# Transformer block, fp32-like matmuls on one core: the first stage written out in a fixed order, and sums over partitions done on four column groups

## The chip, the cores and the metric

The kernel runs on one core of one Trainium2 chip. The metric is the device time in microseconds (us) of one execution; lower is better.

## What is computed

Two layers of a diffusion backbone over 512 latent tokens `x` and 256 context tokens `ctx`, 1024 wide. Cut to what matters here:

```python
silu_c, silu_cc = silu(c), silu(c_ctx)[None]
for i in range(2):                                   # layer 0: attention, layer 1: short conv
    mod   = silu_c  @ ada_w[i] + ada_b[i]            # six vectors of 1024 for the latent tokens
    mod_c = silu_cc @ ada_w[i] + ada_b[i]            # the same for the context
    h  = rmsnorm(x,   norm1_g[i]) * (1 + sc1)  + sh1
    hc = rmsnorm(ctx, norm1_g[i]) * (1 + csc1) + csh1
    y  = diff_attention(h, hc, ...)                  # 8 heads, q, k, v from h; k, v from hc too
    x  = x + g1 * y
    x  = x + g2 * swiglu(rmsnorm(x, norm2_g[i]) * (1 + sc2) + sh2)
return rmsnorm(x, final_g)
```

Only the latent stream is returned, so the context stream is needed for the keys and values of layer 0 alone.

## The kernel before

**Products.** An fp32 operand is split into a high part rounded to fp32r and the fp32r rest (`split`, lines 54 to 56: ACT casts, DVE subtracts), and a product is three fp32r matmuls, high by high, high by low and low by high (`mm3`, lines 78 to 81). Everything stays feature-major: features on partitions, tokens along the free axis.

**First stage** (lines 123 to 313). It loads `x` (four tiles `xn`), `ctx` (two tiles `cn`), the first 2048 columns of `ada_w[0]` (sixteen halves `raw_a`, 512 KB each in two transfers, through a pool of three buffers) and, for each of eight feature blocks k, the 512 columns of `wqkv` that head 0 (q, k) and heads 0 and 1 (v) need (`raw_w`). For each k, `ada0` sums silu(c) and silu(c_ctx) times the block of `ada_w` over all 1024 rows: both halves are split by ACT and DVE into `whi_a` and `wlo_a`, sixteen matmuls `pm` of 256 columns with four weight columns (`cst`) accumulate, ACT copies the four rows to `mr`, two small transposes `pmt` turn them, and DVE makes the gain `A` and shift `m`. `norm_apply` then makes `hx[k]` (`hh`, `hl`) and `hc[k]` (`ch`, `cl`), and the products of block k add to `vps` (v), `qps` and `kps`.

**Attention** (lines 398 to 640). For head 0 `finish_v`, `finish_q` and `finish_k` split v, apply the rotary embedding on DVE (`swq`, `rtq`, `swk`, `rtk`, `qt`, `kt`) and spread q and k over partitions by eight transfers (`qs`, `ks`); then come the score matmuls `S`. Between the heads stand the products of later heads (`psq`, `psk`, `pskc`, `psv`), steps of the modulation vectors (below) and `subnorm`, which sums a head's squares over partitions: four matmuls `pq` with the squares as weights and one column of ones.

**Modulation vectors** (`ada_steps`). The other ten vectors are summed as `acc += silu(c)[k] * ada_w[k rows]` on DVE (tiles `ada`, loads `araw`), then over partitions: the three during attention (`spread_sum` false) by eight one-column matmuls `pada`; the seven during the first FFN (`spread_sum` true) by a split, two times two fp32r matmuls of 512 columns with a matrix of ones, a masked product and a reduction on DVE.

**Order.** The program is written in the order above, but a scheduler that simulates the engines decides where each instruction stands in its engine's queue, and every engine, SP's queue of transfers among them, runs its queue in order. So loads and casts for later heads stand between those of the first stage.

Of the kernel before, what the change touches and what calls it, by code (L numbers as in the profile page):

```python
# [25 lines left out]
def block_kernel(  # L26
# [74 lines left out]
    const.tile([P, 104], F32, name="pad")  # L101
# [20 lines left out]
    for tag, n, bufs in (  # L122
# [3 lines left out]
        + [("sq", 512, 1), ("dg1", 512, 1)]  # L126
# [33 lines left out]

# [38 lines left out]
    def nat_rstd(src, tag, name):  # L199

        nb = len(src)
        ss = ap.tile([P, 8], F32, tag="ss", name=f"ss{name}")
        for t in range(nb):
            for f in range(2):
                junk = ap.tile([P, 512], F32, tag="sq", bufs=1, name=f"junk{name}")
                nc.scalar.activation(
                    junk, src[t][:, f * 512:(f + 1) * 512], AF.Square,
                    accum_out=ss[:, t + 4 * f:t + 4 * f + 1],
                )
# [4 lines left out]
        nc.gpsimd.tensor_tensor(r, v, mhalf[:, :nb], op=ALU.pow)  # L214
        ps = spread(r, nb, "pt", name)
# [17 lines left out]
    def ada0(k, raws):  # L233
        pm = psB.tile([P, 512], F32, tag="pt", name=f"pm{k}")[0:4, 0:256]
        for hf in range(2):
            hi, lo = split_w(raws[hf], 1024, f"a{k}_{hf}")
            for i in range(4):
                kb = 4 * hf + i
                for n, w in enumerate((hi, lo)):
                    nc.tensor.matmul(  # L240
                        pm, cst[:, kb, :], w[:, i * 256:(i + 1) * 256],
                        start=(kb == 0 and n == 0), stop=(kb == DB - 1 and n == 1),
                    )
        mr = ap.tile([4, 256], F32, tag="dg1", bufs=1, name=f"mr{k}")
        nc.scalar.copy(mr, pm)
        pt = psB.tile([P, 512], F32, tag="pt", name=f"pmt{k}")[:, :8].rearrange("p (s c) -> p s c", c=4)
        for s in range(2):
            nc.tensor.transpose(pt[:, s, :], mr[:, s * P:(s + 1) * P], ident[0:4, 0:4])
        nc.vector.reduce_sum(out=m0[:, k], in_=pt.rearrange("p s (m h) -> p s m h", h=2), axis=AX.X)
        nc.vector.tensor_tensor(  # L250
            m0[:, k], m0[:, k], bias0[:, k, :, None].to_broadcast([P, 2, 2]), op=ALU.add
# [4 lines left out]


    XT0 = [ap.tile([P, T], F32, tag=f"Or{k}", bufs=1, name=f"XT{k}") for k in range(DB)]
    rx = nat_rstd(xn, "sw", "x")
    for k in range(0, DB, 2):  # L260
        pt = psB.tile([P, 2, T], F32, tag="S", name=f"ptx{k}")
        for a in range(2):
            for t in range(TB):
                nc.tensor.transpose(pt[:, a, t * P:(t + 1) * P], xn[t][:, (k + a) * P:(k + a + 1) * P], ident)
            nc.vector.tensor_copy(XT0[k + a], pt[:, a, :])
        if k == 0:
            ada0(0, raws0)
    rc = nat_rstd(cn, "ks0", "c")
    ctt = [ap.tile([P, 4, C], F32, tag="araw", name=f"ct{i}") for i in range(2)]
    CT = [ctt[k // 4][:, k % 4, :] for k in range(DB)]  # L270
    for i in range(2):
        pt = psB.tile([P, 4, C], F32, tag="S", name=f"ptc{i}")
        for a in range(4):
            k = 4 * i + a
            for t in range(CB):
                nc.tensor.transpose(pt[:, a, t * P:(t + 1) * P], cn[t][:, k * P:(k + 1) * P], ident)
        for a in (0, 2):
            nc.scalar.copy(ctt[i][:, a:a + 2, :], pt[:, a:a + 2, :])
# [3 lines left out]
    kcps = vps[1][:, 512:768]  # L282
    for k in range(DB):
        raws = raws0 if k == 0 else [load_ada0(k, hf) for hf in range(2)]
        raw = ap.tile([P, 512], F32, tag="e", bufs=3, name=f"raw_w0_{k}")
        qkv = da_wqkv[0, k * P:(k + 1) * P, :].rearrange("p (s c) -> p s c", s=3)
        nc.sync.dma_start(raw[:, 0:256].rearrange("p (s c) -> p s c", s=2), qkv[:, 0:2, 0:P])
        nc.sync.dma_start(raw[:, 256:512], qkv[:, 2, 0:256])
        if k:
            ada0(k, raws)  # L290
        norm_apply(ap, "rt", hx[k], XT0[k], rx, A0[:, k, 0:1], m0[:, k, 0, 0:1], T)
        wh = ap.tile([P, 512], F32R, tag="pth", bufs=3, name=f"w0h_{k}")
        wl = ap.tile([P, 512], F32R, tag="ptl", bufs=3, name=f"w0l_{k}")
        nc.scalar.copy(wh, raw)
# [647 lines left out]
```

## Time and profile before

| | us |
|---|---|
| median of three runs (lowest, highest) | 1350.98 (1350.11, 1352.2) |
| profiled execution | 1350.57 |
| its span, first to last instruction | 1348.8 |
| PE busy in it (share) | 1302.2 (97%) |
| DVE, ACT, POOL busy | 786.4, 501.8, 97.2 |

The span is what the trace covers; 1.8 us of the profiled time lie outside it. A busy PE means that some matmul was in flight, not that it ran at its peak.

### The profile page before, as it was taken

The page shows a single profiled execution, that of the slowest core. Times are in us where ns is not written, and L with a number is a line of the kernel's source. Part 1 is how long each engine was busy: PE and PEld are TensorE (multiplying, and loading weights), DVE is VectorE, ACT ScalarE, POOL GpSimd, SP SyncE. Part 2 cuts the span into 40 slices and gives each one's busy share as a digit, 9 for nine tenths or more (in the row PEclk, how much of TensorE's full clock was granted, in tenths as well). Part 3 has the DMA queues.
Part 4 walks back from the last instruction along what each step waited for, and adds up shares of the span by engine and source line. Part 5 has one row for each costly group of instructions (what it writes and reads, how often), then busy time and mean ns, then how long its engine had stood idle before and what let it go on. Part 6 is the DMA issues. An engine that isn't in the chain of part 4 may idle for free.

```text
span 1348.8 us, 17927 instructions
## 1 busy us (share of the span) xinstructions
PE 1302.2 (97%) x7068; PEld 1120.1 (83%) x7068; DVE 786.4 (58%) x1089; ACT 501.8 (37%) x841; POOL 97.2 (7%) x103
## 2 busy tenths in 40 slices
PE   6788999999999999999999999999999999999997
PEld 5568899999789888888788899888898888888887
DVE  6787989888867677767642265444563333332222
ACT  7534455545556333322222253222452223222122
POOL 2100000000014000000000050000420000000000
PEclk9998999999999999999999999999999999999999
DMA  9865755623532677667633323333233333333321
GB/s 301 259 202 146 207 126 172 156 64 96 153 110 84 184 218 218 207 214 218 210 102 102 101 65 110 94 102 101 79 94 94 99 104 94 94 91 113 100 72 63
DMA packets 238742, 182.79 MB, mean 136 GB/s; under 512 B 6937, under 2 KB 220226, under 8 KB 238658
## 3 DMA queue, kind: packets, MB, share of 16 engines
q1 hardware_dynamic: 238658, 181.65, 45.6%
q8 instruction: 55, 0.90, 0.3%
q14 instruction: 29, 0.24, 0.1%
HBM read 162.75 MB, written 4.19 MB: 124 GB/s over the span
## 4 chain that ended last, share of the span: by engine, by line
PE 82%; DMA 9%; DVE 5%; ACT 2%; issue 1%; SPq 1%; POOL 1%; DVEq 0%; ACTq 0%; POOLq 0%
PE po_fo L81 6%; PE po_fo L79 6%; PE po_fo L80 6%; DMA araw<-in_ada_w_dram 5%; PE pb L80 5%; PE pb L79 5%; PE pb L81 5%; PE pa L80 5%; PE pa L79 5%; PE pa L81 5%; PE S L511 3%; DMA raw_a<-in_ada_w_dram 2%; DVE ada L365 2%; PE pt L532 1%; PE psv L80 1%; PE psv L81 1%
## 5 line engine op out<-in xcount | busy, mean ns | idle before, releaser
L55 ACT CAST whi_f<-raw_f 128x1024 fp32r<-128x1024 f32 x87 | 91.4, 1051 | 232.7 <-issue 118.2
L56 DVE TENSOR_TENSOR wlo_f<-raw_f,whi_f 128x1024 fp32r<-128x1024 f32 x87 | 107.4, 1234 | 77.9 <-ACT whi_f L55 75.0
L56 DVE TENSOR_TENSOR wlo_fo<-raw_fo,whi_fo 128x1024 fp32r<-128x1024 f32 (+1 forms) x48 | 54.5, 1135 | 118.2 <-ACT whi_fo L55 116.8
L79 PE MATMUL po_fo<-uh,whi_fo 128*128 128x512 f32 (+1 forms) x324 | 118.7, 366 | 0.1
L80 PE MATMUL po_fo<-ul,whi_fo 128*128 128x512 f32 (+1 forms) x324 | 118.6, 366 | 0.0
L81 PE MATMUL po_fo<-uh,wlo_fo 128*128 128x512 f32 (+1 forms) x324 | 118.4, 365 | 0.0
L365 DVE SCALAR_TENSOR_TENSOR ada<-araw,sil,ada 128x1024 f32<-128x1024 f32 x70 | 90.1, 1287 | 47.4 <-DMA araw<-in_ada_w_dram 47.2
L55 ACT CAST whi_fo<-raw_fo 128x1024 fp32r<-128x1024 f32 (+1 forms) x48 | 47.1, 981 | 177.6 <-PE po_fo L80 142.3
L784 DVE TENSOR_TENSOR uu<-sl,pb 128x512 f32<-128x512 f32 (+1 forms) x48 | 30.7, 640 | 81.2 <-PE pb L81 76.7
L81 PE MATMUL pb<-h2h,wlo_f 128*128 128x512 f32 (+1 forms) x192 | 71.7, 374 | 0.0
L79 PE MATMUL pa<-h3h,whi_f 128*128 128x512 f32 (+1 forms) x192 | 71.5, 373 | 0.0
L80 PE MATMUL pb<-h2l,whi_f 128*128 128x512 f32 (+1 forms) x192 | 71.4, 372 | 0.0
L79 PE MATMUL pb<-h2h,whi_f 128*128 128x512 f32 (+1 forms) x192 | 71.4, 372 | 0.0
L81 PE MATMUL pb<-h3h,wlo_f 128*128 128x512 f32 (+1 forms) x192 | 71.3, 371 | 0.0
L80 PE MATMUL pb<-h3l,whi_f 128*128 128x512 f32 (+1 forms) x192 | 71.3, 371 | 0.0
L79 PE MATMUL pb<-h3h,whi_f 128*128 128x512 f32 (+1 forms) x192 | 71.3, 371 | 0.0
L81 PE MATMUL pa<-h3h,wlo_f 128*128 128x512 f32 (+1 forms) x192 | 71.3, 371 | 0.0
L80 PE MATMUL pa<-h3l,whi_f 128*128 128x512 f32 (+1 forms) x192 | 71.1, 371 | 0.0
L79 PEld LDWEIGHTS po_fo<-uh,whi_fo 128*128 128x128 f32 x324 | 61.1, 189 | 10.4 <-DVE on L871 0.3
L80 PEld LDWEIGHTS po_fo<-ul,whi_fo 128*128 128x128 f32 x324 | 61.1, 189 | 10.0
L81 PEld LDWEIGHTS po_fo<-uh,wlo_fo 128*128 128x128 f32 x324 | 61.1, 189 | 9.7
L519 ACT ACTIVATE e<-S,mx 128x768 f32<-128x768 f32 x64 | 58.1, 908 | 23.8 <-DVE mx L515 17.9
(337 smaller groups left out, 3462.9 us busy)
## 6 DMA issues: line engine op xcount, KB each, us to landing
raw_f<-in_ffn_w_in_dram SPq DMA_DIRECT2D x88, 512.0 KB, 3.7
araw<-in_ada_w_dram SPq DMA_DIRECT2D x80, 512.0 KB, 4.4
raw_fo<-in_ffn_w_out_dram SPq DMA_DIRECT2D x32, 512.0 KB, 3.6
raw_a<-in_ada_w_dram SPq DMA_DIRECT2D x32, 256.0 KB, 4.6
qs<-qt SPq DMA_DIRECT2D x32, 256.0 KB, 5.0
raw_wv<-in_da_wqkv_dram SPq DMA_DIRECT2D x12, 512.0 KB, 3.3
ks<-kt SPq DMA_DIRECT2D x32, 192.0 KB, 5.0
raw_fo<-in_ffn_w_out_dram SPq DMA_DIRECT2D x16, 384.0 KB, 3.2
```

The source lines that it names most:

```text
L55: nc.scalar.copy(hi, src)
L56: nc.vector.tensor_tensor(lo, src, hi.bitcast(F32), op=ALU.subtract)
L79: nc.tensor.matmul(ps, sh, mh, start=start, stop=False)
L80: nc.tensor.matmul(ps, sh, ml, start=False, stop=False)
L81: nc.tensor.matmul(ps, sl, mh, start=False, stop=stop)
L365: nc.vector.scalar_tensor_tensor(acc, raw, s, acc, op0=ALU.mult, op1=ALU.add)
L511: nc.tensor.matmul(S[:, a:b], q[m][:, j, qb * P:(qb + 1) * P], ks[m][:, a:b], start=(j == 0), stop=(j == 1),)
L519: nc.scalar.activation(em, S[:, :KV], AF.Exp, bias=mx[:, m:m + 1], accum_out=den[:, m, qb:qb + 1])
L532: nc.tensor.transpose(pt[:, i * P:(i + 1) * P], e[0][:, k * P:(k + 1) * P], ident)
L784: nc.vector.tensor_tensor(u, s, pb, op=ALU.mult)
```

## The change

Four parts. (1) `ada0` becomes `ada0_sums` and `ada0_columns`: no split; `cst` holds fp32 weights padded from 2 to 32 columns, and eight plain fp32 matmuls of 256 columns write four groups of 32 PSUM partitions, feature block i of each half to group i; two matmuls with a 0/1 matrix `pick` then add the four groups and turn the result. The raw halves go round nine buffers (the three of `raw` and the six of `whi` and `wlo`). (2) The stage is inside `manual_schedule` for PE, DVE, ACT and SP: its instructions keep the order in which they are written (context products one block behind the latent ones), the loads stand in the order of use, and the transfers that only later stages need are issued after the last load of `raw_w`. Instructions of later stages may still stand between. DVE makes the low part of `raw_w`, which POOL made; ACT copies four of the eight `XT` tiles. (3) `ada_steps` sums over partitions by four fp32 matmuls of 256 columns on four groups, an ACT copy `sada`, and two transposes, in both places. (4) `subnorm` does the same with 128 columns, a copy `sums` and one transpose. `finish_q` and `finish_k` are written ahead of `finish_v`.

```diff
-    def load_ada0(k, hf):
-        raw = wp.tile([P, 1024], F32, tag="raw", name=f"raw_a{k}_{hf}")
+    def load_ada0(i):
+        k, hf = divmod(i, 2)
+        raw = wp.tile([P, 1024], F32, tag=("raw", "whi", "wlo")[i % 3], bufs=nw, name=f"raw_a{k}_{hf}")
...
+    fixed = ExitStack()
+    fixed.enter_context(tc.manual_schedule(engines={
+        mybir.EngineType.PE, mybir.EngineType.DVE, mybir.EngineType.Activation, mybir.EngineType.SP
+    }))
...
-        pm = psB.tile([P, 512], F32, tag="pt", name=f"pm{k}")[0:4, 0:256]
+        pm = psB.tile([P, 512], F32, tag="pt", name=f"pm{k}")[:, 0:256]
         for hf in range(2):
-            hi, lo = split_w(raws[hf], 1024, f"a{k}_{hf}")
             for i in range(4):
-                kb = 4 * hf + i
-                for n, w in enumerate((hi, lo)):
-                    nc.tensor.matmul(
-                        pm, cst[:, kb, :], w[:, i * 256:(i + 1) * 256],
-                        start=(kb == 0 and n == 0), stop=(kb == DB - 1 and n == 1),
-                    )
+                nc.tensor.matmul(
+                    pm[32 * i:32 * i + 32, :], cst[:, 4 * hf + i, :], raws[2 * k + hf][:, i * 256:(i + 1) * 256],
+                    start=(hf == 0), stop=(hf == 1),
+                )
...
+        while len(raws) < min(2 * k + 11, 2 * DB):
+            raws.append(load_ada0(len(raws)))
...
     for k in range(DB):
+        if k + 1 < DB:
+            split_w0(k + 1)
+        mr = ada0_sums(k + 1) if k + 1 < DB and k != 1 else None
         for t in range(TB):
+            values(vps[0], hx, t, k)
+        if mr is not None:
+            ada0_columns(k + 1, mr)
+            latent(k + 1)
         for o, ps in ((0, qps), (P, kps)):
+            columns(k, o, ps, hx)
...
+        if k >= LAG:
+            context_products(k - LAG)
+            context(k - LAG + 1)
...
+    with tc.issue_after(last_w.ins):
...
         for k in range(DB):
             nc.sync.dma_start(xt_dram[k], XT0[k])
...
-        hi, lo = (pool.tile([P, D], F32R, tag="araw", name=f"ada{n}{l}_{j}") for n in "hl")
-        split(hi, lo, acc)
...
+        for g in range(4):
+            nc.tensor.matmul(
+                ps[32 * g:32 * g + 32, 0:256], ones_f[:, 0:32], acc[:, g * 256:(g + 1) * 256],
+                start=True, stop=True,
+            )
+        sums = pool.tile([P, 256], F32, tag="dg1", bufs=1, name=f"sada{l}_{j}")
+        nc.scalar.copy(sums, ps[:, 0:256])
+        for n in range(2):
+            nc.tensor.transpose(ps[:, 256 + n * P:256 + (n + 1) * P], sums[:, n * P:(n + 1) * P], ident)
...
         for t in range(n):
             nc.tensor.matmul(
-                ps[:, t:t + 1], sq[:, t * P:(t + 1) * P], ones_f[:, 0:1], start=True, stop=True
+                ps[32 * t:32 * t + 32, 0:P], ones_f[:, 0:32], sq[:, t * P:(t + 1) * P], start=True, stop=True
             )
+        sums = ap.tile([P, P], F32, tag="sums", bufs=1, name=f"sums{h}")
+        nc.scalar.copy(sums[:32 * n], ps[:32 * n, 0:P])
```

The order moves in three places that matter below. First PE's queue around block 3 of the first stage, before:

```order
L248 MATMUL pmt_528<-ident,mr_526 128x4 x2
L240 MATMUL pm_582<-whi_a_0_583,cst 4x256
L240 MATMUL pm_582<-wlo_a_0_584,cst 4x256
...
L79 MATMUL vps_365<-w0h_538,hh_139 128x256
L80 MATMUL vps_365<-w0l_539,hh_139 128x256
L79 MATMUL qps<-hh_139,w0h_538 128x512
L79 MATMUL kps<-hh_139,w0h_538 128x512
L79 MATMUL vps_366<-w0h_538,ch_155 128x256
L80 MATMUL vps_366<-w0l_539,ch_155 128x256
L240 MATMUL pm_582<-wlo_a_1_596,cst 4x256
```

and of the change, at block 4 (`hh_144`, `hl_145` are its parts):

```order
L260 MATMUL pm_644<-raw_a_0_346,cst 32x256 x4
L260 MATMUL pm_644<-raw_a_1_382,cst 32x256 x4
L79 MATMUL vps_360<-w0h_582,hh_144 128x256
L80 MATMUL vps_360<-w0l_583,hh_144 128x256
L81 MATMUL vps_360<-w0h_582,hl_145 128x256
...
L273 MATMUL pmt_667<-pick,mr_653 128x2 x2
L79 MATMUL qps<-hh_144,w0h_582 128x512
```

The sums of one block stand in a piece ahead of the products of the block before, where they were strewn between them. Second, SP's queue of transfers at the end of the first stage, before (the last `raw_a` and what follows):

```order
L360 DMA araw_2_0_1113<-in_ada_w_dram 128x1024
L153 DMA raw_a_0_897<-in_ada_w_dram 128x4x128 x2
L153 DMA raw_a_1_900<-in_ada_w_dram 128x4x128 x2
L70 DMA raw_wq_1268<-in_da_wqkv_dram 128x8x128
L360 DMA araw_2_1_1149<-in_ada_w_dram 128x1024
L70 DMA raw_wk_1274<-in_da_wqkv_dram 128x8x128
```

and of the change, where `...` stands for seven more `xt_spill` and eight small loads:

```order
L154 DMA raw_a_1_539<-in_ada_w_dram 128x4x128 x2
L70 DMA raw_wq_1136<-in_da_wqkv_dram 128x8x128
L165 DMA raw_w_7_586<-in_da_wqkv_dram 128x2x128
L166 DMA raw_w_7_586<-in_da_wqkv_dram 128x256
L392 DMA rcos<-in_rope_cos_dram 128x512
L396 DMA lamr<-in_da_lambda_dram 128x256
L401 DMA xt_spill<-XT_241 128x512
...
L436 DMA araw_2_0_981<-in_ada_w_dram 128x1024
L70 DMA raw_wk_1142<-in_da_wqkv_dram 128x8x128
L70 DMA raw_wv_0_1255<-in_da_wqkv_dram 128x4x256
L436 DMA araw_2_1_1017<-in_ada_w_dram 128x1024
```

All spills of `XT` and the small loads now stand between the last weights of the first stage and the first `araw`. Third, DVE's queue at the same place, of the change (`hl_149` and `hl_151` are the low parts of blocks 6 and 7, `swq_887` is the first step of q of head 0):

```order
L439 TENSOR_SCALAR ada_2_980<-araw_2_0_981,sil 128x1024
L246 SCALAR_TENSOR_TENSOR hl_149<-na,m_239,hh_148 128x512
...
L441 SCALAR_TENSOR_TENSOR ada_2_980<-araw_2_1_1017,sil,ada_2_980 128x1024
L274 TENSOR_TENSOR m_239<-pmt_777,V_226 128x4
...
L441 SCALAR_TENSOR_TENSOR ada_2_980<-araw_2_2_1077,sil,ada_2_980 128x1024
L246 SCALAR_TENSOR_TENSOR hl_151<-na,m_239,hh_150 128x512
...
L441 SCALAR_TENSOR_TENSOR ada_2_980<-araw_2_3_1113,sil,ada_2_980 128x1024
L477 TENSOR_TENSOR swq_887<-qps,rsin 128x512
```

Four steps of the vector `ada_2` stand ahead of `swq`, one of them ahead of each of the last two low parts; before, six steps stood ahead of it. Between the steps that are shown stand two `raw` casts' subtractions (`wlo_wk`, `wlo_wv_0`) too.

## Rows read from the trace of the kernel before

**Rows 1.** Windows by stage: us and busy us (instructions) per engine, granted clock, DMA share, GB/s.

```profile
0.00:86.00 86.00, 64.09 (x416) 49.88 (x416) 63.54 (x115) 48.67 (x85) 15.52 (x16) 0.98 0.85 267
86.00:108.00 22.00, 15.67 (x73) 13.13 (x73) 16.75 (x30) 5.49 (x11) 0.00 (x0) 0.89 0.71 195
108.00:450.00 342.00, 336.21 (x2252) 307.32 (x2253) 288.51 (x478) 177.19 (x358) 27.14 (x31) 0.99 0.48 132
450.00:1348.80 898.80, 886.27 (x4330) 749.78 (x4328) 417.56 (x468) 270.43 (x389) 54.57 (x56) 1.00 0.41 123
```

**Rows 2.** Groups of instructions up to 108 us: busy us, mean ns, idle time before.

```profile
L56 DVE TENSOR_TENSOR wlo_a<-raw_a,whi_a 128x1024 fp32r<-128x1024 f32 x16 | 20.0, 1252 | 8.1 <-ACT whi_a L55 7.9
...
L55 ACT CAST whi_a<-raw_a 128x1024 fp32r<-128x1024 f32 x16 | 16.6, 1044 | 12.1 <-DMA raw_a<-in_ada_w_dram 11.4 <-PE pm L240 0.6
```

**Rows 3.** Waits of SP's queue up to 110 us: in total, times, longest.

```profile
SPq L153 <- DVE wlo_a L56: 7.2, 5, 2.3
```

**Rows 4.** Windows of the loading, columns as in the first group.

```profile
4.00:28.00 24.00, 16.37 (x99) 12.10 (x100) 16.00 (x35) 18.18 (x41) 7.46 (x5) 1.00 1.03 345
28.00:48.00 20.00, 16.61 (x110) 13.48 (x108) 14.46 (x22) 12.25 (x18) 3.21 (x2) 0.91 0.94 279
```

**Rows 5.** Timeline of PE: start, us, line, shapes, count, [idle before].

```profile
29.51 0.40 PE L81 MATMUL kps<-hh,w0l 128*128 128x512 f32 x1
29.74 0.28 PE L79 MATMUL vps<-w0h,ch 128*128 128x256 f32 x1
29.86 0.28 PE L80 MATMUL vps<-w0l,ch 128*128 128x256 f32 x1
29.97 0.28 PE L240 MATMUL pm<-whi_a,cst 128*4 128x256 f32 x1
30.09 0.28 PE L81 MATMUL vps<-w0h,cl 128*128 128x256 f32 x1
```

**Rows 6.** Timeline of PE later: plain fp32 matmuls and transposes.

```profile
127.04 0.49 PE L532 MATMUL pt<-ident,e 128*128 128x128 f32 x3
...
128.06 1.62 PE L372 MATMUL pada<-ones_f,ada 128*128 128x1 f32 x14
...
418.48 1.02 PE L586 MATMUL pn<-nsq,ones_f 128*128 128x256 f32 x4
```

**Rows 7.** Instructions on the tile `pada` in the first FFN: ns min, median, max.

```profile
L385 PE MATMUL pada<-adah,ones_r x14: 397/404/496, 464.6 to 681.0; 128*128 128x512 f32 x14
```

**Rows 8.** Timeline of SP's queue: start, us in the queue, transfer, count.

```profile
18.68 0.85 SPq L326 DMA_DIRECT2D xt_spill<-XT  x2
...
66.99 0.34 SPq L360 DMA_DIRECT2D araw<-in_ada_w_dram  x1
...
96.65 3.22 SPq L420 DMA_DIRECT2D qs<-qt  x4
99.92 3.90 SPq L420 DMA_DIRECT2D ks<-kt  x4
```

**Rows 9.** Timeline of DVE: steps of the vector `ada`, then head 0.

```profile
58.24 0.75 DVE L363 TENSOR_SCALAR ada<-araw,sil 128x1024 f32<-128x1024 f32 x1 [0.96 <-DMA araw<-in_ada_w_dram]
...
70.90 1.69 DVE L365 SCALAR_TENSOR_TENSOR ada<-araw,sil,ada 128x1024 f32<-128x1024 f32 x1 [0.56 <-DMA araw<-in_ada_w_dram]
...
82.94 1.28 DVE L365 SCALAR_TENSOR_TENSOR ada<-araw,sil,ada 128x1024 f32<-128x1024 f32 x1 [1.50 <-DMA araw<-in_ada_w_dram]
...
87.28 0.68 DVE L408 TENSOR_TENSOR swq<-qps,rsin 128x512 f32<-128x512 f32 x1
...
99.44 0.69 DVE L56 TENSOR_TENSOR kt<-rtk,kt 128x512 fp32r<-128x512 f32 x1
```

**Rows 10.** Timeline of PE at the first scores.

```profile
107.98 2.90 PE L511 MATMUL S<-ks,qs 128*128 128x512 f32 x8 [3.71 <-issue]
```

**Rows 11.** Windows at the first scores, columns as in the first group.

```profile
107.00:110.00 3.00, 2.02 (x6) 1.76 (x7) 2.13 (x5) 1.80 (x3) 0.00 (x0) 0.50 0.28 90
110.00:115.00 5.00, 5.00 (x30) 4.86 (x29) 4.55 (x7) 1.76 (x4) 0.00 (x0) 0.68 0.74 166
```

More of the change, by code (lines that the diff above doesn't have):

```diff
@@ L268, in block_kernel, with split_w0, values @@
-    rc = nat_rstd(cn, "ks0", "c")
+    W0 = {}
+    def split_w0(k):
+        raw, W0[k, "dma"] = raw0[k]
+        wh = ap.tile([P, 512], F32R, tag="pth", bufs=3, name=f"w0h_{k}")
+        wl = ap.tile([P, 512], F32R, tag="ptl", bufs=3, name=f"w0l_{k}")
+        split(wh, wl, raw)
+        W0[k] = wh, wl
+        if len(raw0) < DB:
+            raw0.append(load_w0(len(raw0)))
+    def values(ps, h, t, k):
+        wh, wl = W0[k]
+        mm3(
+            ps[:, t * 256:(t + 1) * 256], h[k][0][:, t * P:(t + 1) * P], h[k][1][:, t * P:(t + 1) * P],
+            wh[:, 256:512], wl[:, 256:512], k == 0 and t % 2 == 0, k == DB - 1 and t % 2 == 1,
+        )
@@ new lines, in columns, with latent, context, context_products @@
+    def columns(k, o, ps, h):
+        wh, wl = W0[k]
+        mm3(ps, wh[:, o:o + P], wl[:, o:o + P], h[k][0], h[k][1], k == 0, k == DB - 1)
+    def latent(k):
+        norm_apply(ap, "rt", hx[k], XT0[k], rx, A0[:, k, 0:1], m0[:, k, 0, 0:1], T)
+    def context(k):
+        norm_apply(ap, "rt", hc[k], CT[k], rc, A0[:, k, 1:2], m0[:, k, 0, 1:2], C)
+    def context_products(k):
+        for t in range(CB):
+            values(vps[1], hc, t, k)
+        columns(k, P, kcps, hc)
+    XT0 = [ap.tile([P, T], F32, tag=f"Or{k}", bufs=1, name=f"XT{k}") for k in range(DB)]
@@ L269, in block_kernel @@
+    nc.vector.tensor_copy(XT0[6], ptx[6])
+    nc.vector.tensor_copy(XT0[0], ptx[0])
+    r = rstd_of(ssx, TB, "x")
+    for k in (2, 4):
+        nc.vector.tensor_copy(XT0[k], ptx[k])
+    for k in (7, 1, 3, 5):
+        nc.scalar.copy(XT0[k], ptx[k])
+    rx = spread_out(r, TB, "sw", "x")
+    split_w0(0)
+    mr = ada0_sums(0)
+    ada0_columns(0, mr)
+    latent(0)
     ctt = [ap.tile([P, 4, C], F32, tag="araw", name=f"ct{i}") for i in range(2)]
     CT = [ctt[k // 4][:, k % 4, :] for k in range(DB)]
[L271 to L278, printed above, removed]
@@ L282, in block_kernel @@
     kcps = vps[1][:, 512:768]
+    ptc = vps[1].rearrange("p (a c) -> p a c", c=C)
+    LAG = 1
     for k in range(DB):
[L284 to L294, printed above, removed]
-        nc.gpsimd.tensor_tensor(wl, raw, wh.bitcast(F32), op=ALU.subtract)
-        for t in range(TB):
-            mm3(
-                vps[0][:, t * 256:(t + 1) * 256],
-                hx[k][0][:, t * P:(t + 1) * P], hx[k][1][:, t * P:(t + 1) * P],
-                wh[:, 256:512], wl[:, 256:512], k == 0 and t % 2 == 0, k == DB - 1 and t % 2 == 1,
-            )
@@ L303, in block_kernel @@
-        for o, ps in ((0, qps), (P, kps)):
-            mm3(ps, wh[:, o:o + P], wl[:, o:o + P], hx[k][0], hx[k][1], k == 0, k == DB - 1)
-        norm_apply(ap, "rt", hc[k], CT[k], rc, A0[:, k, 1:2], m0[:, k, 0, 1:2], C)
-        for t in range(CB):
-            mm3(
-                vps[1][:, t * 256:(t + 1) * 256],
-                hc[k][0][:, t * P:(t + 1) * P], hc[k][1][:, t * P:(t + 1) * P],
-                wh[:, 256:512], wl[:, 256:512], k == 0 and t % 2 == 0, k == DB - 1 and t % 2 == 1,
-            )
```

184 lines of the change are left out of this document (105 added, 79 removed).

## The prediction

> **What bounds the kernel now.** I read the windows by stage first [rows 1]. From 108 us, where the first scores start, to the end PE has a matmul in flight for 336.2 of 342.0 us and then for nearly all of the remaining 898.8 us, while DVE stays below it: there the time is PE's work, and whoever hands PE a microsecond less or starts it a microsecond earlier gains it. Ahead of that stands a stretch of 108 us in which PE is busy for 64.1 of 86 and 15.7 of 22 us. This is the stage that the change rewrites. What ends last in it shows in three views. SP's queue waits 7.2 us for DVE's `wlo_a` [rows 3]: a raw half can't be loaded until the split has freed its buffer. The transfers run at 345 GB/s up to 28 us and at 279 up to 48 us [rows 4]. After that stage comes the chain of head 0 on DVE: `swq` at 87.28, the last `kt` ending at 100.13 (99.44 + 0.69) [rows 9], eight transfers whose last issue ends at 103.82 [rows 8], the first score at 107.98, after 3.71 us in which PE does nothing [rows 10].
>
> So the question is when the first score starts in the changed kernel, what PE has behind it by then, and what the new sums cost PE afterwards.
>
> **The sums on PE.** In the kernel before, a 256-column fp32r matmul takes 0.12 us from start to start and a 512-column one 0.23 [rows 5]. A plain fp32 matmul of 256 columns is two records; four records of `pn` take 1.02 us, and with 0.38 us for the last one alone the spacing is (1.02 - 0.38) / 3 = 0.214 us, so 0.43 us for one matmul [rows 6]. Four of them cost 1.71 us if the groups run one after the other, and 0.43 if all four run at once. No row of before shows two column groups at work, so both ends stay. I take a value between: matmuls start in order, the second record of a group needs the same columns as the first and must wait for it, and the next group's first record can run beside it. That makes five slots in place of eight, 1.07 us. Per block of `ada0` (eight matmuls, nine slots) this is 1.9 us, with ends 0.9 and 3.4; before it was 16 x 0.115 = 1.8.
>
> Later sums. The seven of the first FFN took four 512-column matmuls [rows 7], 4 x 0.23 = 0.9 us; now 1.07 plus two transposes at 0.11 ((0.49 - 0.27) / 2 [rows 6]), 1.3 us: +0.4 each, +2.9. The three during attention took 16 records at 0.105 [rows 6], 1.7 us; now 1.3: -1.1. The nine of `subnorm` took 0.8 us (eight records) and take 5 x 0.107 + 0.11 = 0.65: -1.1 for them, with two half-sized. Sum on PE: +0.9 us (one after the other: +9.7; all at once: -8.3). The splits, masked products and reductions that go from DVE and ACT in the FFN lie beside a PE that is never short of work there [rows 1]; I cost them at nothing, and the ACT copy that now stands between sums and transposes has some 20 matmuls of the FFN to hide behind (without them PE would stand for the copy, some 0.3 us each by a quarter of the 1.04 us cast of 1024 columns [rows 2], 3 us for the ten).
>
> Changing between matmuls of 128 and of 4 weight columns costs nothing that shows: `vps`, `pm`, `vps` start at 29.86, 29.97, 30.09, the usual 0.12 [rows 5]. The Trainium skill (TensorEngine Tiling (Array Packing), section Key Properties) says that changing the tiling mode drains the engine. The trace doesn't show it at this place; what it would cost is a rival below.
>
> **The first stage.** Gone: 16 ACT casts and 16 DVE subtractions, 16.6 and 20.0 us [rows 2], and with them the wait for buffers, since PE's sums alone now free a raw half, and nine halves fit. Added: eight subtractions of 512 columns on DVE, at half of 1.25 us each 5 us, taken from POOL, hidden under the loads. Products of a block cost PE 21 x 0.12 + 6 x 0.23 = 3.9 us as before. With 1.9 us of sums a block is 5.8 us of PE. Its loads are 1.05 MB of `raw_a` and 0.26 MB of `raw_w`: at 0.31 MB per us (between the two windows) 4.2 us. PE is slower than the transfers, from about 13 us on, when the last `x` and the first block (3.2 MB) are in.
>
> But the queues hold a tail that the stage didn't have. `raw_wq` waits for the sums of block 4, whose columns I put at 45 us: from 13, five sums, three blocks of products, transposes of `ctx` (3 us), and the first blocks' chains through ACT and DVE (some 5 us). By bytes (13.4 MB ahead of it) it could be issued at about 42, so this is no earlier. Its split stands in ACT's and DVE's order ahead of the parts of block 4: PE stops there for about 4 us. Behind `raw_wq` SP has 20 issues (two of `raw_w`, `rcos`, `lamr`, eight spills, eight small loads) at 0.42 us [rows 8], 8.5 us, with some waiting for transfers in flight: the first `araw` is issued at about 55 us and lands 3.9 us later (66.99 to 70.90 [rows 8, 9]), at 59.
>
> From there a chain sets the end. Each of the next three `araw` takes the same buffer, which the DVE step before must free, and those steps stand ahead of the low parts of blocks 6 and 7 and of `swq`. The same chain stands in the kernel before: 58.24 to 82.94 us are four links [rows 9], 6.2 us each (the two outer values I take as 5.2 and 7.4). So: 59 + 3 x 6.2 + 1.2 (the step itself) = 78.8 us for `swq`, against 87.28. PE's products end under this chain.
>
> From `swq` to the last `kt` DVE did 12.85 us of work with two `ada` steps; now four steps stand there: +2.4, so `kt` ends at 78.8 + 15.2 = 94.0. From there to the first score it was 7.85 us, with four issues of `ks` in 3.90; two of the four now stand ahead: -1.95, so 5.9. The first score starts at 99.9 us, 8.1 earlier. Ahead of it PE now has all of `psv_0`, 24 x 0.12 = 2.9 us, which stood behind it; this fits under the chain, and is credited in full because PE is short of time afterwards.
>
> Sum, against the profiled execution (1350.57, near the median of 1350.98): 1350.6 - 8.1 - 2.9 + 0.9 = 1340.5 us. Up to 3 us more could come from the clock: it is granted at 0.50, the lower of its two levels (1.2 of 2.4 GHz), for the 3 us behind the gap ahead of the first score, and at 0.68 on the mean for 5 more [rows 11], 3 x 0.50 + 5 x 0.32 = 3.1 us of PE. A shorter gap may not lower it; I leave it out of the sum and in the range.
>
> **Rivals.**
> *All four groups at once.* In its favour: the outputs lie in different column groups. Against: two records per matmul in one queue. Sums of a block cost 0.9 us, so the stage follows the transfers: 17.2 MB up to the first `araw` at 0.31 MB per us end at about 57, the score at 97.9, -10.1; with -2.9 and -8.3 this is 1329 us. The Trainium skill (TensorE: Matmul & The Clock Gate, section Measured speedup vs the span model) gives 2.38 times for three column groups; that is for single matmuls side by side, and no run here shows it yet.
>
> *One group after the other: slower than before.* Sums of a block 3.4 us, 7.3 with its products. Block 4's sums end 5 x 1.5 us later, less some 2 that the stalls swallow: first `araw` at 64.5, `swq` at 84.3, score at 105.4, -2.6; with -2.9 and +9.7 on PE 1355 us. It decides from about 1.8 slots per pair of records on, where the PE work alone eats the earlier start.
>
> *The chain eats the start.* The spills' writes and small loads land late (first `araw` at 62) and a link takes 7.4: 62 + 22.2 + 1.2 = 85.4, score at 106.5, nothing else won: 1350 us. In its favour: the longest link of before. Against: SP's queue is emptier behind the spills than before.
>
> *A drain at each change.* If each change of tiling costs what a matmul's record is longer than its spacing (0.28 - 0.12 = 0.16), 19 later sums with two changes each cost 6.1 us: 1347. The rows above speak against it. It is what the Trainium skill's rule on changes of mode, named above, would mean here.
>
> **How the numbers follow.** Forecast 0.43, all at once 0.20, one after the other 0.20, the chain 0.12, the drain 0.05. A measurement of this kernel can tell about 0.2% (2.7 us) from no change. Faster by more: the first two and most of the drain, with a little of the chain, 0.68; within: most of the chain and an edge of the serial case, 0.12; slower: 0.20. The range takes in both prices of the groups with the clock at the low end: 1327 to 1356. The forecast's own, with links of 5.2 to 7.4 and the clock, is 1334 to 1345.
>
> **What the profile will show.** Records of `pm` from group to group: pairs that start 0.21 us apart (right), all within 0.05 (all at once) or eight in a row without overlap (serial). The first `araw` near 59 us, `ada` steps some 6 us apart, `swq` near 79, the first score near 100. PE busy in the FFN as before. I am wrong if the first score moves by less than 5 us, or if the time from it to the end changes by more than 5.

## The result, and the profile after

The changed kernel takes 1358.99 us (median of four executions, 1358.43 to 1359.57) where the kernel before took 1351.01 on the same chip: a ratio of 1.0066, interval 1.0047 to 1.0085. It is slower by 0.5 to 0.9%. Forecast was 1340.5 us in a range of 1327 to 1356, with 0.20 on slower. The profiled execution took 1359.57 us, 1357.8 of them span; of before, 1350.57 and 1348.8.

First the windows by stage of the changed kernel, columns as in [rows 1], from the start to the first score (107.3), then to the first norm ahead of the first FFN (407.5), to the last one ahead of the second (983.9) and to the end.

```profile
0.00:107.30 107.30, 79.03 (x528) 64.96 (x528) 61.80 (x125) 41.39 (x83) 2.42 (x8) 0.91 0.87 260
107.30:407.50 300.20, 288.90 (x1904) 254.65 (x1904) 251.19 (x430) 154.54 (x319) 13.30 (x15) 0.99 0.48 131
407.50:983.90 576.40, 565.31 (x2907) 479.66 (x2907) 295.87 (x333) 181.68 (x276) 55.32 (x59) 1.00 0.46 140
983.90:1357.80 373.90, 366.06 (x1782) 309.85 (x1780) 131.39 (x154) 108.74 (x165) 12.07 (x14) 1.00 0.31 93
```

The same for the kernel before, with limits at the same events.

```profile
0.00:108.00 108.00, 79.76 (x489) 63.01 (x489) 80.28 (x144) 54.16 (x95) 15.52 (x16) 0.96 0.82 252
108.00:406.00 298.00, 292.49 (x1936) 265.75 (x1936) 253.08 (x432) 152.63 (x308) 13.97 (x15) 0.99 0.50 134
406.00:974.90 568.90, 563.90 (x2863) 481.55 (x2864) 321.56 (x360) 186.16 (x276) 55.62 (x59) 1.00 0.47 142
974.90:1348.80 373.90, 366.10 (x1782) 309.80 (x1780) 131.42 (x154) 108.82 (x165) 12.13 (x14) 1.00 0.31 93
```

Length less PE's busy time is the time in which PE has no matmul in flight. It went from 28.2 to 28.3 us ahead of the first score, from 5.5 to 11.3 in the attention, from 5.0 to 11.1 in the first FFN, and stayed at 7.8 behind it. So 0.7 us are won in the first stage, 2.2 lost in the attention, 7.5 in the first FFN. Nothing that the change does to PE's own work explains it: PE is busy for 2.9 us less.

The first stage up to head 0, on DVE (timeline, as [rows 9]):

```profile
62.40 0.75 DVE L439 TENSOR_SCALAR ada<-araw,sil 128x1024 f32<-128x1024 f32 x1
...
67.24 1.28 DVE L441 SCALAR_TENSOR_TENSOR ada<-araw,sil,ada 128x1024 f32<-128x1024 f32 x1 [0.56 <-DMA araw<-in_ada_w_dram]
...
73.72 1.28 DVE L441 SCALAR_TENSOR_TENSOR ada<-araw,sil,ada 128x1024 f32<-128x1024 f32 x1 [2.94 <-DMA araw<-in_ada_w_dram]
...
79.01 1.27 DVE L441 SCALAR_TENSOR_TENSOR ada<-araw,sil,ada 128x1024 f32<-128x1024 f32 x1
80.20 0.68 DVE L477 TENSOR_TENSOR swq<-qps,rsin 128x512 f32<-128x512 f32 x1
...
94.83 0.69 DVE L56 TENSOR_TENSOR kt<-rtk,kt 128x512 fp32r<-128x512 f32 x1
```

`swq` starts at 80.20 and the last `kt` ends at 95.52, where [rows 9] have 87.28 and 100.13: the first stage is 4.6 us ahead here. Then SP's queue and the first score (as [rows 8] and [rows 10]):

```profile
88.96 3.48 SPq L489 DMA_DIRECT2D qs<-qt  x4
92.54 0.54 SPq L436 DMA_DIRECT2D araw<-in_ada_w_dram  x1
93.12 1.46 SPq L489 DMA_DIRECT2D ks<-kt  x2
94.69 0.77 SPq L70 DMA_DIRECT2D raw_wv<-in_da_wqkv_dram  x1
95.55 1.20 SPq L436 DMA_DIRECT2D araw<-in_ada_w_dram  x1
96.84 1.11 SPq L489 DMA_DIRECT2D ks<-kt  x2
```

```profile
107.34 2.90 PE L580 MATMUL S<-ks,qs 128*128 128x512 f32 x8 [5.12 <-DMA ks<-kt]
```

The last `ks` is issued by 97.95, 5.9 us earlier than before (103.82), and PE starts the scores 9.4 us after that, where it was 4.2. The view of the tile `ks` around head 0 gives the time from issue to landing of the transfer that PE waits for, first in the changed kernel, then before:

```profile
DMA to landing us min/median/max: 10.6/10.6/10.6
```

```profile
DMA to landing us min/median/max: 5.4/5.4/5.4
```

Three loads of 512 KB (two `araw`, one `raw_wv`) stand between `qs` and the last two `ks`; before, all eight transfers followed one another. From 96 to 108 us the transfers run at 222 to 262 GB/s and their engines are full (windows, last two columns share and GB/s):

```profile
96.00:100.00 4.00, 1.83 (x15) 1.63 (x14) 3.81 (x7) 1.66 (x2) 0.00 (x0) 1.00 1.00 222
100.00:104.00 4.00, 2.22 (x19) 2.01 (x17) 0.77 (x2) 0.00 (x0) 0.00 (x0) 1.00 1.08 262
```

The 1.57 MB of the three loads take some 6.5 us at that rate; the `ks` transfers land 5.2 us later after their issue than before.

In the first FFN, PE's waits and the timeline of PE at one vector (in brackets the idle time ahead of a row):

```profile
PE pada L450 <- DVE ada L441: 7.7, 7, 2.1
```

```profile
504.65 0.39 PE L80 MATMUL pa<-h2l,whi_f 128*128 128x512 f32 x1
506.85 0.64 PE L450 MATMUL pada<-ada,ones_f 128*32 128x256 f32 x8 [1.81 <-DVE ada L441]
507.42 0.54 PE L81 MATMUL pa<-h2h,wlo_f 128*128 128x512 f32 x1
507.76 0.63 PE L79 MATMUL pa<-h2h,whi_f 128*128 128x512 f32 x1
...
513.90 0.38 PE L457 MATMUL pada<-ident,sada 128*128 128x128 f32 x2
```

DVE's last addition for these sums (timeline of DVE) had waited for its load:

```profile
505.42 1.28 DVE L441 SCALAR_TENSOR_TENSOR ada<-araw,sil,ada 128x1024 f32<-128x1024 f32 x1 [1.35 <-DMA araw<-in_ada_w_dram]
```

For each of the seven vectors PE comes to the sums before DVE has made the last addition. Each wait holds all products behind it, and after this one they run slower for some 4 us (0.63 us a matmul, not 0.39; the granted clock is 0.96 on the mean from 500 to 540 us, and 1.00 in the kernel before). The transposes stand 5.4 to 7 us behind the sums, so the ACT copy is hidden, as forecast. What is late is the load: from 440 to 600 us DVE waits for `araw` for 49.3 us in all, and for 29.0 in the kernel before. The windows of the same 160 us of FFN, the changed kernel first, then before:

```profile
440.00:600.00 160.00, 154.41 (x723) 124.46 (x723) 110.63 (x119) 46.19 (x65) 0.00 (x0) 0.99 0.81 257
```

```profile
440.00:600.00 160.00, 160.00 (x716) 132.50 (x716) 111.29 (x121) 51.49 (x66) 0.00 (x0) 1.00 0.69 212
```

The transfers run at 257 GB/s in place of 212. The program takes four steps of the modulation vectors per block of the FFN; a vector had eleven steps (eight additions, with the split in the step of the last, then three for the sums and the reduction) and has eight now. So its loads come denser, and the sums stand in the step of the last addition, where they stood behind it.

### The profile page after: what moved, and what is told of

The parts are those of the page before. It is cut to its first block, busy times and chain, and to the rows that moved or that the text cites. A ratio compares the mean times of both kernels' runs of the same rounds, so it can differ in the third digit from the quotient of the medians.

```text
span 1357.8 us, 17908 instructions
## 1 busy us (share of the span) xinstructions
PE 1299.3 (96%) x7117; PEld 1109.1 (82%) x7117; DVE 740.2 (55%) x1040; ACT 486.3 (36%) x841; POOL 83.1 (6%) x95
## 4 chain that ended last, share of the span: by engine, by line
PE 74%; DMA 10%; DVE 9%; ACT 3%; issue 3%; POOL 1%; SPq 0%; DVEq 0%; ACTq 0%; POOLq 0%
DMA araw<-in_ada_w_dram 8%; PE po_fo L79 6%; PE po_fo L80 6%; PE po_fo L81 6%; PE pb L80 4%; PE pb L81 4%; PE pb L79 4%; PE pa L81 4%; PE pa L80 4%; PE pa L79 4%; PE S L580 3%; DVE ada L441 2%; PE pt L601 1%; PE psc L80 1%; PE psb L81 1%
```

## Experiments

My theory after these rows: three losses, none of them PE work. (a) In the FFN the sums stand too close behind loads that have become too dense. (b) The early start of head 0 is eaten by three loads in the transfers' queue. (c) In the attention, `subnorm` or the three vectors there make PE wait 5.8 us more. Rivals: the first stage itself slows what follows; the sums on column groups cost by themselves; an earlier first score is worth nothing, since the attention waits for DVE.

All results in one table: length of a stretch and, behind the stroke, PE's idle time in it (windows: length less PE busy), the median, and the ratio to the kernel before on the same chip with its interval.

| kernel | to first score | attention | first FFN | median | ratio (interval) |
|---|---|---|---|---|---|
| before | 108.0 / 28.2 | 298.0 / 5.5 | 568.9 / 5.0 | 1351.0 | 1 |
| changed | 107.3 / 28.3 | 300.2 / 11.3 | 576.4 / 11.1 | 1359.0 | 1.0066 (1.0047 to 1.0085) |
| first_only | 106.5 / 26.9 | 295.5 / 5.2 | 568.8 / 5.2 | 1347.7 | 0.9987 (0.9976 to 0.9997) |
| later_only | 105.9 / 27.1 | 303.6 / 10.2 | 578.1 / 12.8 | 1364.3 | 1.0119 (1.0101 to 1.0138) |
| pace | 109.6 / 26.0 | 299.7 / 11.3 | 567.4 / 4.1 | 1353.0 | 1.0017 (1.0007 to 1.0027) |
| late | 106.0 / 26.9 | 301.6 / 10.9 | 569.4 / 6.1 | 1353.2 | 1.0024 (1.0012 to 1.0035) |
| ks_first | 98.0 / 22.8 | 305.6 / 11.1 | 575.4 / 10.1 | 1357.2 | 1.0057 (1.0041 to 1.0072) |
| ada_late | 86.9 / 16.4 | 320.3 / 22.7 | 577.7 / 12.5 | 1364.6 | 1.0107 (1.0088 to 1.0126) |
| ks_late | 99.5 / 20.8 | 304.7 / 11.1 | 572.3 / 7.3 | 1349.0 | 0.9990 (0.9978 to 1.0003) |
| pool_v | 100.3 / 25.5 | 303.7 / 11.4 | 568.8 / 5.5 | 1350.9 | 1.0004 (0.9990 to 1.0017) |
| old_ada | 107.9 / 25.3 | 306.4 / 11.7 | 567.6 / 4.2 | 1356.0 | 1.0047 (1.0034 to 1.0060) |
| two_tiles | 109.9 / 27.5 | 300.4 / 10.0 | 570.3 / 6.7 | 1352.9 | 1.0015 (1.0002 to 1.0028) |
| long_way | 107.8 / 25.5 | 306.4 / 8.3 | 567.4 / 3.9 | 1357.3 | 1.0055 (1.0038 to 1.0072) |
| first_ks | 100.2 / 21.1 | 297.0 / 6.2 | 570.7 / 5.9 | 1341.5 | 0.9935 (0.9924 to 0.9947) |
| first_ks_ffn | 99.6 / 21.7 | 299.2 / 6.7 | 568.0 / 3.4 | 1341.9 | 0.9939 (0.9927 to 0.9951) |
| all_fixed | 97.3 / 23.4 | 305.0 / 10.1 | 566.8 / 3.4 | 1345.9 | 0.9969 (0.9958 to 0.9980) |

The stretches are of one execution each, and executions of one kernel lie up to 10 us apart (the profiled ones of ks_late and two_tiles are the slowest of theirs), so times are compared by the ratios.

**Which half loses: first_only and later_only.** Each undoes the other half. In the changed kernel:

```diff
-                ps[32 * g:32 * g + 32, 0:256], ones_f[:, 0:32], acc[:, g * 256:(g + 1) * 256],
+                nc.tensor.matmul(ps, ones_r, w[:, hf * 512:(hf + 1) * 512], start=(i == 0), stop=(i == 1))
...
-                ps[32 * t:32 * t + 32, 0:P], ones_f[:, 0:32], sq[:, t * P:(t + 1) * P], start=True, stop=True
+                ps[:, t:t + 1], sq[:, t * P:(t + 1) * P], ones_f[:, 0:1], start=True, stop=True
```

> The changed kernel with the sums of ada_steps and of subnorm as in the kernel before: only the first stage is new. Theory (the loss in the first FFN comes with the later sums alone): the stretch from the end of the attention to the second FFN takes 568 to 570 us as before, not 576, and the time is 1351 to 1353 us. On the attention two views differ: if its 5.8 us of added PE waits came with the later sums too, PE waits 5 to 7 us in it and the time is 1346 to 1348; if they come with the first stage, 10 to 12 us and 1351 to 1353. Rival (the new sums are harmless and something in the memory plan slows the FFN): 576 us there, 1357 to 1359.

The kernel before, with the new `ada_steps` and `subnorm`:

> The kernel before with the sums of ada_steps and subnorm as in the changed kernel: the first stage is old. Theory: the stretch of the first FFN takes 575 to 577 us in place of 568.7, with 6 to 8 us of waits of pada for ada; time 1356 to 1359. Rival (the loss needs the new first stage): 568 to 571 us there, 1349 to 1352.

The first stage alone is faster than before, just measurably (0.9987); the later sums alone cost 1.2%. Idle time in the attention and in the FFN sits with the later sums, 5.2 and 5.2 us without them, 10.2 and 12.8 with them. The waits of later_only in the FFN:

```profile
PE pada L372 <- DVE ada L365: 9.4, 6, 2.7
```

So the loss needs nothing of the new first stage, and that rival falls. later_only was expected at 1356 to 1359, which left out the attention: that takes 5.6 us more than in the kernel before, and the FFN 9.2.

**Why in the FFN: pace and late.** late adds one empty step ahead of the sums (first lines), pace three behind them (last lines):

```diff
         m = mod[l][:, 8 * j:8 * j + 8]
+        if spread_sum:
+            yield
...
         yield
+        if spread_sum:
+            for _ in range(3):
+                yield
```

> The changed kernel with three empty steps behind each vector of the first FFN, so that a vector takes eleven steps as before and not eight; the sums still stand in the same step as the last addition. Theory (the rate): eight steps in place of eleven put the loads of ada_w four to a block of the FFN, the transfers run at 260 GB/s where they ran at 209, the last addition of each vector is late, and PE stands for it 7 times, 7.7 us. Then the waits of pada for ada fall below 2 us, the rate goes back to about 210 GB/s, and the time to 1351 to 1353 us. Rival (the place): sums queued right behind the last addition are waited for at any rate; 5 to 8 us of waits stay, 1357 to 1359 us.

> The changed kernel with one empty step between the last addition of a vector of the FFN and its sums: nine steps to a vector, loads nearly as dense as in the changed kernel. Theory (the rate): the last addition is as late as before against the order that was planned, so half or more of the 7.7 us of waits stay, 1355 to 1359 us. Rival (the place): a step between them is what the split was in the kernel before; the waits fall below 2 us, 1351 to 1353 us.

The waits in the FFN, first of pace, then of late:

```profile
PE pada L450 <- DVE ada L441: 0.7, 1, 0.7
```

```profile
PE pada L451 <- DVE ada L441: 2.7, 2, 2.4
```

Either repair gives back some 6 us, at 238 and 249 GB/s; in pace I had expected about 210. I had set them against each other; both views hold in part. The wait needs dense loads and sums placed right behind the last addition, and taking away either is enough.

**Why the start is no earlier: ks_first and ada_late.** In the first, the loads of vector 3 and the second `raw_wv` are queued behind the last `ks` of head 0; in the second, those of vector 2 as well. `behind` puts what it encloses after that transfer in SP's queue (ks_first; ada_late has `(l, j) in ((0, 2), (0, 3))`).

```diff
+            with behind((l, j) == (0, 3)):
                 nc.sync.dma_start(raw, ada_w[l, k * P:(k + 1) * P, j * D:(j + 1) * D])
```

> The changed kernel with three loads of 512 KB (araw_3_0, araw_3_1, raw_wv) queued behind the four ks transfers of head 0. Theory: the ks transfers took up to 10.6 us to land because these loads were ahead of them in the queue; behind them they land within 5.5 us as before, and the first score starts at 100 to 102 us in place of 107.3. If PE is the bound from there on, the time falls by 5 to 6 us, to 1353. Rival (the rest of the attention waits for DVE, which is busy for 251 of 300 us in it): the first score comes earlier, but the end of the attention moves by less than 2 us: 1357 to 1359. Second rival (the loads are not what ks waits for): first score at 106 or later, 1359.

> The changed kernel with all loads of the vectors 2 and 3 (and the second raw_wv) queued behind the ks transfers of head 0, so that no step of them stands on DVE ahead of swq. Theory: the four steps ahead of swq wait for their loads and hold the low part of block 7, which holds PE; without them swq comes at 73 to 75 us, the last kt at 84, the first score at 88 to 91, 17 us earlier. The eight steps (9.5 us of DVE) go into the attention; with DVE the bound there 7 us are left, 1350 to 1353; with PE the bound all 17, 1342. Rival: the chain of head 0 and not the steps sets the start; first score later than 100, 1356 to 1360.

The first score of ks_first, and of ada_late with its `swq`:

```profile
98.03 1.84 PE L587 MATMUL S<-ks,qs 128*128 128x512 f32 x8 [1.82 <-DMA ks<-kt]
```

```profile
86.89 0.86 PE L587 MATMUL S<-ks,qs 128*128 128x512 f32 x4
```

```profile
72.01 0.67 DVE L478 TENSOR_TENSOR swq<-qps,rsin 128x512 f32<-128x512 f32 x1
```

The loads were what `ks` waited for: 98.0 us in place of 107.3. But the time hardly moves: the ratio is 1.0057 after 1.0066, within both intervals, and 1357.2 us lies where this run's rival had it. Of the 9.3 us, 3.9 are PE work that stood ahead of the first score and stands behind it now (PE busy ahead of it 79.03 and 75.16), and PE's idle time falls by 5.5. ada_late shows the limit: scores 20 us earlier, and the attention 20 us longer. Its 1364.6 us lie outside all that I had expected (1342, 1350 to 1353, 1356 to 1360). The eight additions of vector 2 now stand on DVE beside the first heads, and PE waits 9.0 us there for exponentials. That DVE sets this pace is argued here, not shown.

**Both repairs, and DVE relieved: ks_late and pool_v.** ks_late joins ks_first and late. pool_v also makes the low parts of `raw_wv` on POOL:

```diff
+        if name[:2] == "wv":
+            nc.scalar.copy(hi[:, :w], raw[:, :w])
+            nc.gpsimd.tensor_tensor(lo[:, :w], raw[:, :w], hi[:, :w].bitcast(F32), op=ALU.subtract)
```

> The changed kernel with both repairs: three loads behind the ks transfers of head 0, and one empty step between the last addition and the sums in the FFN. Theory (the two losses are separate): 1357.2 less the 5.8 us that the empty step gave alone, 1350 to 1352; first score at 97 to 99, FFN stretch at 568 to 570 us. Rival (what is gained in one place is given back in the other): 1353 or more.

> As ks_late, with the low parts of the twelve raw_wv tiles made on POOL in place of DVE (15 us of DVE work taken out of the attention, in which DVE is busy for 253 of 306 us). Theory (the attention gives an earlier start back because DVE is its bound): PE's waits in it fall from 11 to under 6 us and the time to 1344 to 1347. Rival (its pace is a chain from matmul to maximum to exponential to split, not the sum of DVE's work): the waits stay at 9 to 12 us, and the time is within 2 us of ks_late. Second rival (POOL is too slow or slows DVE): later than ks_late by more than 2 us.

Neither repair gives back what the other gains: 1349.0, about as before (0.9990, where the two gains added would leave 1.0015). Relief by POOL moved nothing: 11.4 us idle in the attention, and 11.1 in ks_late. It is no clean test of DVE, though: DVE had 10 subtractions of 1.2 us less there and was still busy for 257.3 us, where it was 253.4 in ks_late, as its other work became slower beside POOL (last section). Whether DVE sets the attention's pace is left open.

**What costs in the attention: old_ada, two_tiles, long_way.** old_ada is the changed kernel with the old sums of `ada_steps` alone; two_tiles is old_ada with the transposed sums of `subnorm` in a tile of their own; long_way is first_only with a copy and a second pass that change no value, and no column groups (second diff).

```diff
-        pq = ps[:, P:P + 32 * n]
+        pq = psB.tile([P, 512], F32, tag="pt", name=f"pqt{h}")[:, :32 * n]
```

```diff
+        nc.scalar.copy(sums, ps[:, :n])
+        pq = ps[:, P:P + n]
+        nc.tensor.matmul(pq, ident, sums, start=True, stop=True)
```

> The changed kernel with the sums of ada_steps as before, in the attention and in the FFN; subnorm keeps its new sums. The undoing of both took PE's waits in the attention from 11.3 to 5.2 us. Theory (subnorm's copy and transpose cost them): the waits in the attention stay at 9 to 12 us, the FFN stretch is 568 to 570 us, the time 1351 to 1353. Rival (the three sums of ada in the attention cost them): waits of 5 to 6 us and a time of 1346 to 1348.

> As old_ada, with the transposed sums of subnorm in a second tile of the pool pt, so that neither tile is held through the copy on ACT and the transpose. Theory (with its sums, copy and transpose in one tile, subnorm holds one of the two pt buffers for 5 to 7 us per head, where it held it 1.1, and the transposes of p wait for that buffer): the waits of PE in the attention fall from 11.7 us to 5 to 7 and the time from 1356.0 to 1348 to 1350. Rival (the longer way of a head's scale, through ACT and a second pass on PE, holds up what comes after it, whatever buffer it uses): waits of 10 to 12 us, 1355 to 1357.

> As first_only, whose sums of subnorm are the old one-column matmuls, with a copy on ACT and a second pass through PE put behind them that change no value: the way of the new subnorm without column groups. Theory (the longer way is what costs: the buffer of pt held through it, and the scale of O that comes later): PE's waits in the attention rise from 5.2 to 9 to 12 us and the time from 1347.7 to 1354 to 1357, as in old_ada. Rival (the plain fp32 sums on column groups disturb PE): 5 to 6.5 us of waits, 1347 to 1349.

`subnorm` costs it: old_ada, with its new sums, has 11.7 us of idle time in the attention and a ratio of 1.0047; first_only, without them, 5.2 us and 0.9987, some 8 us less. The price is not the same everywhere: with the new sums of the vectors beside it (changed, pace and late) the attention takes 299.7 to 301.6 us, 306.4 in old_ada and 295.5 in first_only, so the losses don't simply add. The timeline of PE in old_ada at head 6 shows one such place:

```profile
387.52 0.43 PE L634 MATMUL pq<-sq,ones_f 128*32 128x128 f32 x8
388.95 0.97 PE L589 MATMUL S<-ks,qs 128*128 128x512 f32 x4 [1.00 <-ACT e L597]
389.76 0.27 PE L640 MATMUL pq<-ident,sums 128*128 128x128 f32 x1
389.87 0.49 PE L610 MATMUL pt<-ident,e 128*128 128x128 f32 x3
391.96 0.55 PE L610 MATMUL pt<-ident,e 128*128 128x128 f32 x3 [1.61 <-DVE sv L643]
```

The transposes `pt` of the softmax wait for `sv`, which reads the sums of `subnorm` from one of the two buffers of the pool `pt`. From the first `pq` to the end of `sv` that buffer is held for 5.3 to 7.1 us in the six heads up to 360 us; in the kernel before it was mostly 1.1. A tile for each half of the way (two_tiles) gives back some 4 of the 8 us by the ratios, less than I had expected. That PE stands for the buffer is only a small part of it: the waits for `sv` come to 1.9 us in old_ada and to 0.2 in the changed kernel and in long_way, and two_tiles, which has none, still has 10.0 us of idle time, where I had expected 5 to 7. long_way, with the copy and the second pass but no column groups, has the same 306.4 us of attention as old_ada, and a ratio as high: the longer way is enough for the loss, without column groups. Of its 10.9 us over first_only 3.1 are idle time and 7.8 a PE that is busy for longer, at a granted clock of 0.97 on the mean where first_only had 0.99. How much of the way's cost is the buffer and how much the later scale of O stays open.

**A faster kernel: first_ks, first_ks_ffn, all_fixed.** The new first stage with the three loads behind `ks` and all later sums as before; the same with the new sums in the FFN, in eleven steps; the whole change with all repairs.

> The new first stage with all later sums as before, and the three loads behind the ks transfers of head 0. Theory (an earlier first score is kept where the attention's PE waits are short): first score at 97 to 100, PE's waits ahead of it fall from 26.9 to 21 us and stay near 5 in the attention, so 1342 to 1344. Rival (the attention gives it back): attention's waits rise to 9 or more, 1346 to 1349.

> As first_ks, with the new sums in the FFN alone, in eleven steps to a vector with one empty step ahead of the sums. Theory (given the place and the rate of the old sums, the new ones cost PE no wait and save four 512-column matmuls less 0.6 and 0.4 us each): within 2 us of first_ks, FFN stretch at 566 to 569 us. Rival (plain fp32 sums on column groups cost by themselves): 3 us or more above first_ks.

> The whole changed kernel with the repairs: three loads behind the ks transfers of head 0, eleven steps to a vector of the FFN with one empty step ahead of its sums, subnorm on two tiles. Theory (the three losses found are all): PE's waits near those of first_ks_ffn (21.7, 6.7 and 3.4 us), 1341 to 1343. Rival (subnorm's new sums cost by their longer way): 1348 to 1351, as ks_late.

first_ks beats both kernels: 0.9935. The windows of its attention and FFN:

```profile
100.20:397.20 297.00, 290.81 (x1937) 264.35 (x1937) 252.76 (x434) 151.93 (x308) 15.81 (x15) 1.00 0.51 140
397.20:967.90 570.70, 564.84 (x2864) 483.00 (x2865) 321.44 (x360) 186.17 (x276) 55.27 (x59) 1.00 0.47 141
```

Here the earlier start is kept: the ratio falls by 0.0052 from first_only, some 7 us, for 6.3 in the first score. A part of this is the clock, which the prediction left out of its sum. The windows of the 8 us behind the first score, of first_ks and then of first_only:

```profile
100.20:108.20 8.00, 7.99 (x59) 7.55 (x60) 7.80 (x15) 3.34 (x8) 0.00 (x0) 1.00 1.01 309
106.50:114.50 8.00, 8.00 (x42) 7.61 (x43) 5.19 (x11) 3.42 (x8) 0.00 (x0) 0.65 0.91 229
```

PE stood idle for 1.27 us right ahead of the score in first_ks and for 4.42 in first_only (timelines of PE); the granted clock behind it is 1.00 and 0.65, which is 8 x 0.35 = 2.8 us of PE. Against it stand the 2.9 us of `psv_0`, which PE has behind the score here and ahead of it in first_only.

The new sums in the FFN neither help nor harm once their place and pace are right. all_fixed is faster than the kernel before, but 4 us behind first_ks_ffn; its attention still has 10.1 us of idle time, so the third loss is only partly repaired.

## Why the prediction was wrong

Of the 19.1 us between the forecast and the profiled execution 7.4 lie ahead of the first score (0.7 us earlier, not 8.1) and 11.7 behind it (9.7 us lost, not 2.0 won).

**The first stage had the right mechanism, and its number some luck.** `swq` at 78.8 (80.20 measured), last `kt` at 94.0 (95.52). The chain did set it: without the four steps `swq` starts at 72.01 (ada_late). But two errors offset each other: the first `araw` was issued at 57.88, not 55, and its step started at 62.40, not 59 (3.4 us late), while the links were 4.8, 6.5 and 5.3 us, not 6.2 each (2.0 us less in all).

**Column groups: the term was mis-sized, the rival right.** I took pairs, 1.07 us for four matmuls and 1.9 a block. The timeline of PE at one block:

```profile
44.58 0.28 PE L81 MATMUL vps<-ch,w0l 128*128 128x256 f32 x1
44.79 1.07 PE L260 MATMUL pm<-raw_a,cst 128*32 128x256 f32 x16
45.79 0.39 PE L79 MATMUL vps<-w0h,hh 128*128 128x256 f32 x1
46.02 0.28 PE L80 MATMUL vps<-w0l,hh 128*128 128x256 f32 x1
```

Sixteen records of 0.38 us within 1.07: (1.07 - 0.38) / 15 = 0.046 us apart, all four groups at once. A block costs 1.0 us, a later sum 0.57 (506.85 to 507.42 above) and 0.23 for its transposes (the matmuls around them start at 513.66 and 514.35, less two usual steps of 0.23), so 0.8 and not 1.3. The rival's 1329 us did not follow: its first `araw` was to land at about 57 us, and DVE's step on it starts at 62.40. A change of tiling does show here, where [rows 5] showed none for four weight columns: 0.09 us on entry (0.21 for 0.12) and 0.11 on leaving (0.23 for 0.12). The Trainium skill (TensorEngine Tiling (Array Packing), section Key Properties) has such a drain; here it is too small to matter. The recorded sum for the later sums is also off by 0.2 us: +2.9, -1.1 and -1.1 make +0.7, not +0.9; nothing hangs on it.

**The step that failed first: later sums, "+0.9 us", and "I cost them at nothing".** I priced the splits and the copy by their engines' time, beside a PE that is never short of work. What they also did was to hold a step of the program and with it the distance between a vector's loads and its sums. Without them the FFN became 7.5 us longer, and pace and late gave it back. In `subnorm`, for which I had a gain of 1.1 us, the copy and the transpose cost some 8 us alone (old_ada beside first_only); long_way shows that the longer way is enough for it, and what in that way costs stays open beyond the 4 us that a second tile gives back.

**The second: "from there to the first score ... two of the four now stand ahead: -1.95, so 5.9".** It took 11.8 us (95.52 to 107.34). I counted SP's issues of `ks`, and not what lay ahead of them among the transfers: the listing of SP's queue would have shown `araw_3_0`, `raw_wv` and `araw_3_1` there. The step is worth some 7 us (first_only to first_ks, by the ratios).

**The credit for `psv_0` held** where the attention was not disturbed: it takes 295.5 us in first_only, 2.5 less than before; 2.9 were credited.

With the three loads moved and the later sums as before, first_ks has 1341.5 us and its first score at 100.2; forecast were 1340.5 and 99.9. That the times agree so well is partly chance: `psv_0` (2.9 us, in the sum) stands behind the score there, and the clock's gain of about as much was not in the sum. The sign came from the later sums, which I had as the smallest term. I named the right alarms (a first score that moves by less than 5 us; it was 0.7; and a change of over 5 us behind it; it was 9.7) and had no rival for either cause.

## What to carry to other kernels

Work that is removed from an engine off the critical path may have set the distance between a load and its use: look for what then stands directly behind the slowest arrival in the queue of the busiest engine, and leave a step between. When a transfer on the critical path is issued, count the bytes queued ahead of it, not the issues. Sums that take fewer PE cycles but an extra hop through another engine hold their PSUM buffer for the hop and give their results later: price the hop, and not the cycles alone. Here it cost 8 us, of which a second tile gave back about half.

## What the runs showed that I had not expected

Plain fp32 matmuls of 32 weight columns on four column groups run at once, two records each: eight records at 0.046 us are 0.37 us for what would take 1.71 one after the other by the spacing of `pn`, 0.57 with the changes of tiling counted, three times faster. The Trainium skill (TensorE: Matmul & The Clock Gate, section Measured speedup vs the span model) gives 2.38 times for three groups; these rows agree in kind.

Subtractions on POOL hold up DVE. The view of the tile `e` in the attention (times in ns, least, median and most), first ks_late, then pool_v:

```profile
L604 DVE SCALAR_TENSOR_TENSOR e<-e,rr,e x32: 997/1010/1019, 107.7 to 386.4; 128x768 f32<-128x768 f32 x32
```

```profile
L608 DVE SCALAR_TENSOR_TENSOR e<-e,rr,e x32: 1005/1018/3142, 111.1 to 385.8; 128x768 f32<-128x768 f32 x32
```

The one of 3.14 us began while a subtraction of POOL's was under way (timelines of POOL and DVE, pool_v):

```profile
128.63 2.72 POOL L64 TENSOR_TENSOR wlo_wv<-raw_wv,whi_wv 128x1024 fp32r<-128x1024 f32 x1 [5.65 <-PE S L592]
129.02 3.14 DVE L608 SCALAR_TENSOR_TENSOR e<-e,rr,e 128x768 f32<-128x768 f32 x1
```

It ended 0.81 us behind POOL's end (132.16 after 131.35). So one of 1.0 us took up to 3.1 while POOL's took 2.5 us each (10 of them, 25.3 us); DVE's `mx`, which reads PSUM, kept its 0.95. The Trainium skill (SBUF — State Buffer, section SBUF: two separate sides) says that the two engines share a pair of ports as an exclusive lock, and these rows agree.
